# Forty-six instead of forty-one key blocks of a PEER layer sent through DRAM, and the row schedule set to match

## The chip, the core and the metric

One NeuronCore of a Trainium2 chip runs the whole kernel as a single program. Its engines are TensorE (PE in the profile; PEld is its weight load), VectorE (DVE), ScalarE (ACT), GpSimd (POOL) and SyncE (SP, which only issues transfers); each takes its instructions in order from a queue of its own, and they wait for each other and for DMA transfers through semaphores. The metric is the device time of one execution in microseconds (us), the median of several runs.

## The reference, cut to what matters

The kernel computes two transformer blocks on 512 tokens of width 1024; the change touches only the last layer of the second block, a PEER layer (a mixture of 16,384 experts of one neuron each). For every token it picks 128 experts with gates `gb`, and computes

```
u_sel = jnp.take(peer_u, eb, axis=0)              # rows of peer_u, 16384 x 1024
z     = jnp.einsum('td,tkd->tk', hb, u_sel)
act   = jax.nn.gelu(z, approximate=False) * gb
y2    = jnp.einsum('tk,tkd->td', act, jnp.take(peer_v, eb, axis=0))
```

The kernel treats the 512 tokens in two ways. For the first 384 it does not gather: it multiplies with all 16,384 experts, whose gates are zero where an expert was not picked. For the last 128 tokens it gathers the 128 rows of `peer_u` and of `peer_v` of each token.

## The kernel before

The 16,384 experts are 128 blocks ("keys") `a` of 128 experts.

**First product** (`zed(a)`, L1950). z of block `a` for 384 tokens: 24 matmuls of 128x384 into one PSUM tile `acc` (two buffers), eight steps of three (`mm3`, L121, which splits fp32 operands into a high and a low part), with a `yield` after each step. The weight comes through `weight()` (L108): SP loads `wraw` (512 KB, L105), ACT makes the high part `whi` (L117), DVE or POOL the low part `wlo` (L118). Each of the three has four slots, shared by all weights in the order of the program. ACT evicts `acc` through Gelu: for `a` below NR = 128 - ND into one of NZ = 17 tiles `zg` that stay on the chip (L1959), for the ND last blocks into `z_out` (L1962), which SP stores to DRAM as `p_zd` (L1974).

**Gates.** For each group of 16 tokens `peer_gates` (L1891) makes a dense tile `stage` of gates (128 x 128 x 16) and queues its store to DRAM, `p_gd`, 24 stores of 1 MB in all.

**What runs ahead.** The generator `zeds` (L1976) computes the ND blocks of the DRAM route and then the first NZ: 58 first products, 464 steps. `peer_pick` draws 64 + 56 + 28 + 28 = 176 steps between its instructions, `peer_gates` 276, and what is left, 12 steps, runs after the gates in the loop at L2026. Each start of a new product first loads the weight of the next one (L1981) and then issues the stores that have queued up (L1983); the last `p_gd` store is among them.

**The loop over the 128 blocks** (L2074). `fetch(a)` (L2043) brings the gates: every eighth block ACT's queue issues `gt`, 1.5 MB read back from `p_gd`, which waits for the stores. Then POOL multiplies z with the gates (`hid`, L2054), ACT and DVE split it (`hid_h` L2059, `hid_l` L2060), and the **second product** is 18 matmuls of 128x512 (`y`, six PSUM tiles that accumulate over all 128 blocks) against a block of `peer_v`, also through `weight()`. For `a` from NR on, z is read back from `p_zd` (`z_in`, L2052). As long as `a + NZ < NR`, each pass also computes the first product of block `a + NZ`, since `zg[a % NZ]` has just come free. So the loop has a first part of NR - NZ = 70 passes with both products and a second of 58 with the second product alone.

**Rows.** Each pass also handles rows of the 128 gathered tokens: POOL gathers `gu` (a row of `peer_u` per token) and `gv` (of `peer_v`), 512 KB each (L1994), DVE does the dot product (L2003) and the weighted sum into `y3` (L2035). `upto` (L2040) spreads the 128 rows: FAST = 110 of them over the first part of the loop, the rest over the second.

All instructions are ordered by a planner that simulates the engines from a cost model; the order of the program text is the priority, and `issue_after` holds an instruction behind another. The order in each engine's queue is fixed before the kernel runs.

Of the kernel before, what the change touches and what calls it, by code (L numbers as in the profile page):

```python
# [25 lines left out]
class Net:  # L26
# [1906 lines left out]
    def peer_layer(self, x, mod):  # L1933
        nc, A = self.nc, self.A
        V = nc.vector
        NZ, ND, FAST, LEAD = 17, 41, 110, 20
        xr = self.dram.tile([T, D], F32, name="p_xr")
        gd = self.dram.tile([24, 128, 128, 16], F32, name="p_gd")
        zd = self.dram.tile([ND, 128, 384], F32, name="p_zd")
# [360 lines left out]
```

## Time and profile before

| | us |
|---|---|
| median of 3 runs | 3050.35 |
| the runs | 3048.65, 3050.35, 3057.16 |
| the profiled execution | 3048.28 |
| its span in the trace | 3046.4 |
| mean granted TensorE clock | 0.954 |
| PE / DVE / ACT / POOL busy | 2748.0 / 2342.8 / 1400.3 / 1235.6 |

All places in time below are us from the start of that span. The first products run from 1845 us on (first eviction to `z_out`), the gates end near 2176, the loop runs from there to about 3005. Busy time of PE counts a pipelined matmul to its modelled end, so counts of matmuls in a stretch say more than its busy time. PEclk is the granted clock: 1.00 is 2.4 GHz, 0.5 is 1.2 GHz. "DMA share" is the mean busy share of the core's 16 DMA engines.

### The profile page before, as it was taken

How to read it: one execution, taken by the hardware profiler on the slowest of the kernel's cores; microseconds unless marked ns; L12 is line 12 of the kernel's file. 1: busy time of each engine (PE TensorE's matmuls, PEld its weight loads, DVE VectorE, ACT ScalarE, POOL GpSimd, SP SyncE). 2: the span in 40 equal slices, each digit the busy share in tenths (PEclk: the TensorE clock that was granted, in tenths of full speed). 3: DMA queues.
4: the chain of work that ended last, by engine and by line, in shares of the span. 5: the costliest groups of instructions: out<-in, count | busy, mean ns of one | idle time of the engine just before them, and what ended most of it. 6: DMA issues, size and time to landing. Idle time of an engine off the chain costs nothing.

```text
span 3046.4 us, 42674 instructions
## 1 busy us (share of the span) xinstructions
PE 2748.0 (90%) x14989; PEld 2234.8 (73%) x14989; DVE 2342.8 (77%) x4500; ACT 1400.3 (46%) x2688; POOL 1235.6 (41%) x894
## 2 busy tenths in 40 slices
PE   2899978898889798899898899999899999999996
PEld 2777556676556566576676588999889999998885
DVE  7998457768974686777974699998598888886667
ACT  3354437744554574432333533688533333333332
POOL 3111017743211484004941245120177777774332
PEclk9999889999899799998998999999999999999998
DMA  6776158933634797221011124796699999997782
GB/s 217 245 231 198 42 212 293 330 132 125 190 126 151 244 341 241 90 73 28 5 59 57 69 83 128 228 316 219 214 363 350 351 356 351 349 351 270 247 265 98
DMA packets 234337, 627.53 MB, mean 206 GB/s; under 512 B 33180, under 2 KB 95948, under 8 KB 230648
## 3 DMA queue, kind: packets, MB, share of 16 engines
q1 hardware_dynamic: 134416, 434.54, 42.0%
q0 software_dynamic: 45120, 154.42, 14.4%
q10 hardware_dynamic: 54568, 35.66, 4.0%
q8 instruction: 122, 2.00, 0.3%
q14 instruction: 111, 0.91, 0.1%
HBM read 564.94 MB, written 63.37 MB: 206 GB/s over the span
## 4 chain that ended last, share of the span: by engine, by line
PE 47%; DVE 13%; DMA 3%; issue 2%; ACT 1%; POOL 0%; POOLq 0%; DVEq 0%; ACTq 0%; SPq 0%
PE acc L124 7%; PE acc L125 7%; PE acc L126 7%; PE y L126 6%; PE y L125 6%; PE y L124 5%; DVE s_y L1367 1%; DMA wraw<-in_moe_w_gu_dram 1%; PE S L1922 1%; PE tr L1922 1%; DVE wlo L118 1%; DMA wraw<-in_moe_w_dn_dram 1%; DVE s_y L1526 1%; DVE wc L1550 1%; DVE t L1774 1%
## 5 line engine op out<-in xcount | busy, mean ns | idle before, releaser
L118 DVE TENSOR_TENSOR wlo<-wraw,whi 128x1024 fp32r<-128x1024 f32 x442 | 620.2, 1414 | 202.9 <-ACT whi L117 198.7
L117 ACT ACTIVATE whi<-wraw 128x1024 fp32r<-128x1024 f32 (+1 forms) x552 | 576.6, 1050 | 415.8 <-PE acc L125 254.3
L124 PE MATMUL acc<-h_hi,whi 128*128 128x384 f32 (+1 forms) x1328 | 475.8, 359 | 12.2 <-ACT z_out L1962 7.5
L126 PE MATMUL acc<-h_hi,wlo 128*128 128x384 f32 (+1 forms) x1328 | 466.6, 351 | 2.2 <-DVE wlo L118 2.2
L125 PE MATMUL acc<-h_lo,whi 128*128 128x384 f32 (+1 forms) x1328 | 468.1, 353 | 0.0
L118 POOL TENSOR_TENSOR wlo<-wraw,whi 128x1024 fp32r<-128x1024 f32 (+1 forms) x110 | 278.8, 2542 | 325.8 <-ACT whi L117 317.7
L124 PE MATMUL y<-whi,hid_h 128*128 128x512 f32 x768 | 299.8, 391 | 8.0 <-ACT hid_h L2059 8.0
L126 PE MATMUL y<-whi,hid_l 128*128 128x512 f32 x768 | 303.0, 395 | 4.2 <-DVE hid_l L2060 4.2
L125 PE MATMUL y<-wlo,hid_h 128*128 128x512 f32 x768 | 302.4, 394 | 0.0
L1994 POOL DMA_INDIRECT gu<-in_peer_u_dram,e x128 | 196.0, 1531 | 243.2 <-DVE gu L2003 172.5
L124 PEld LDWEIGHTS acc<-h_hi,whi 128*128 128x128 f32 x1328 | 251.5, 190 | 30.4 <-ACT z_out L1962 8.4
L126 PEld LDWEIGHTS acc<-h_hi,wlo 128*128 128x128 f32 x1328 | 251.1, 189 | 16.7 <-DVE wlo L118 2.5
L1994 POOL DMA_INDIRECT gv<-in_peer_v_dram,e x128 | 200.1, 1563 | 155.1 <-DVE stage L1927 105.6
L125 PEld LDWEIGHTS acc<-h_lo,whi 128*128 128x128 f32 x1328 | 251.5, 189 | 15.7 <-issue 0.8
L2059 ACT ACTIVATE hid_h<-hid 128x384 fp32r<-128x384 f32 x128 | 67.1, 524 | 286.6 <-PE y L125 263.5
L2035 DVE SCALAR_TENSOR_TENSOR y<-gv,pz,y 128x1024 f32<-128x1024 f32 x128 | 183.5, 1434 | 0.7 <-DMA gv<-in_peer_v_dram,e 0.6
L182 DVE SCALAR_TENSOR_TENSOR ada_w<-ada_w,silu 128x1024 f32<-128x1024 f32 x138 | 174.3, 1263 | 7.8 <-DMA ada_w<-in_w_ada_dram 7.8
L124 PEld LDWEIGHTS y<-whi,hid_h 128*128 128x128 f32 x768 | 145.0, 189 | 38.0 <-ACT hid_h L2059 8.4
L126 PEld LDWEIGHTS y<-whi,hid_l 128*128 128x128 f32 x768 | 145.1, 189 | 33.9 <-DVE hid_l L2060 4.6
L125 PEld LDWEIGHTS y<-wlo,hid_h 128*128 128x128 f32 x768 | 145.0, 189 | 31.1 <-DVE wlo L118 0.3
L2003 DVE SCALAR_TENSOR_TENSOR gu<-gu,hrow 128x1024 f32<-128x1024 f32 x128 | 162.7, 1272 | 5.4 <-DMA gu<-in_peer_u_dram,e 5.4
L124 PE MATMUL acc<-whi,h_hi 128*128 128x256 f32 x480 | 140.6, 293 | 28.4 <-ACT whi L117 18.7
(671 smaller groups left out, 6231.5 us busy)
## 6 DMA issues: line engine op xcount, KB each, us to landing
ada_w<-in_w_ada_dram SPq DMA_DIRECT2D x144, 512.0 KB
wraw<-in_moe_w_gu_dram SPq DMA_DIRECT2D x128, 512.0 KB
wraw<-in_peer_ut_dram SPq DMA_DIRECT2D x128, 512.0 KB
wraw<-in_peer_v_dram SPq DMA_DIRECT2D x128, 512.0 KB
wraw<-in_moe_w_dn_dram SPq DMA_DIRECT2D x64, 512.0 KB
p_gd<-stage SPq DMA_DIRECT2D x24, 1024.0 KB
gt<-p_gd ACTq DMA_DIRECT2D x16, 1536.0 KB
wraw<-in_fox_w_in_dram SPq DMA_DIRECT2D x24, 512.0 KB
```

Of the source, the lines that this page charges most:

```text
L117: nc.scalar.activation(hi[:, :w], r[:, :w], AF.Copy)
L118: self.low = eng.tensor_tensor(lo[:, :w], r[:, :w], hi[:, :w].bitcast(F32), op=OP.subtract).ins
L124: mm(out=out, lhsT=l[0], rhs=r[0], start=start, stop=False)
L125: mm(out=out, lhsT=l[0], rhs=r[1], start=False, stop=False)
L126: mm(out=out, lhsT=l[1], rhs=r[0], start=False, stop=stop)
L182: V.scalar_tensor_tensor(r, r, 1.0, c, op0=OP.mult, op1=OP.mult, accum_out=m)
L1367: V.scalar_tensor_tensor(acc[:, c, :], *tap(n), acc[:, c, :], op0=OP.mult, op1=OP.add)
L1922: nc.tensor.matmul(out=pt[:, t * 128:(t + 1) * 128], lhsT=a2[:, b * 4 + t, :], rhs=a1[:, b * 4 + t, :], start=True, stop=True)
L1994: nc.gpsimd.indirect_dma_start(out=u, out_offset=None, in_=src[:, :], in_offset=bass.IndirectOffsetOnAxis(ap=e3[:, k:k + 1], axis=0))
L2003: V.scalar_tensor_tensor(u, u, 1.0, hrow, op0=OP.mult, op1=OP.mult, accum_out=z8[b][:, k % 8:k % 8 + 1])
L2035: V.scalar_tensor_tensor(y3, vs.pop(k), z8[k // 8][:, k % 8:k % 8 + 1], y3, op0=OP.mult, op1=OP.add)
L2059: nc.scalar.activation(hh, hid, AF.Copy)
```

## The change

ND goes from 41 to 46, and FAST from 110 to 104.

```
-        NZ, ND, FAST, LEAD = 17, 41, 110, 20
+        NZ, ND, FAST, LEAD = 17, 46, 104, 20
```

So NR = 128 - ND goes from 87 to 82, `p_zd` holds 46 blocks, the generator has 63 first products (504 steps), of which `peer_pick` and `peer_gates` draw 452 as before; 52 are left for the loop at L2026. The first part of the main loop has 65 passes instead of 70, the second 63 instead of 58.

## Rows read from the trace of the kernel before

**Rows 1.** Busy time by stretch: stretch, us, PE, PEld, DVE, ACT, POOL, PEclk, DMA share, GB/s

```profile
2050.00:2150.00 100.00, 100.00 (x689) 100.00 (x688) 83.41 (x87) 81.99 (x217) 3.58 (x3) 1.00 0.62 221
...
2180.00:2190.00 10.00, 7.47 (x41) 6.83 (x39) 2.92 (x4) 2.50 (x3) 0.00 (x0) 1.00 0.86 263
2190.00:2200.00 10.00, 3.51 (x8) 2.82 (x9) 2.89 (x3) 0.90 (x2) 4.64 (x4) 0.52 0.39 117
2200.00:2210.00 10.00, 5.84 (x27) 4.67 (x25) 4.61 (x5) 1.59 (x2) 8.44 (x9) 0.97 1.03 370
2210.00:2220.00 10.00, 10.00 (x41) 8.46 (x40) 7.94 (x9) 3.54 (x6) 7.62 (x6) 0.83 1.03 402
...
2260.00:2300.00 40.00, 40.00 (x206) 36.53 (x205) 34.69 (x40) 13.81 (x20) 30.05 (x21) 1.00 1.00 366
...
2600.00:2700.00 100.00, 100.00 (x508) 90.95 (x508) 81.60 (x94) 35.38 (x50) 73.06 (x50) 1.00 0.99 352
...
2900.00:2950.00 50.00, 50.00 (x220) 41.03 (x219) 33.62 (x29) 18.20 (x26) 19.43 (x16) 1.00 0.88 281
```

**Rows 2.** All waits of PE between 2160 and 2230 us: total, times, longest

```profile
PE y L124 <- ACT hid_h L2059: 8.0, 1, 8.0
PE y L126 <- DVE hid_l L2060: 4.2, 1, 4.2
PE acc L124 <- ACT whi L117: 1.0, 1, 1.0
```

**Rows 3.** Timeline around the loop's start: start us, duration, instruction [idle before <-releaser]

```profile
2173.82 0.83 PE L1922 MATMUL tr<-a,a 128*128 128x128 f32 x6
...
2176.17 0.33 SPq L1974 DMA_DIRECT2D p_gd<-stage  x1
...
2178.23 1.06 ACT L117 ACTIVATE whi<-wraw 128x1024 fp32r<-128x1024 f32 x1 [3.57 <-PE acc L125]
...
2182.25 0.38 ACTq L2046 DMA_DIRECT2D gt<-p_gd  x1
...
2186.71 1.06 ACT L117 ACTIVATE whi<-wraw 128x1024 fp32r<-128x1024 f32 x1 [2.60 <-PE acc L125]
2187.82 0.44 PE L124 MATMUL acc<-h_hi,whi 128*128 128x384 f32 x1 [0.97 <-ACT whi L117]
...
2194.89 0.99 POOL L2054 TENSOR_TENSOR hid<-x,gt 128x384 f32<-128x384 f32 x1 [27.88 <-DMA gt<-p_gd]
...
2196.03 0.99 POOL L1994 DMA_INDIRECT gu<-in_peer_u_dram,e  x1
...
2196.47 0.56 DVE L2060 TENSOR_TENSOR hid_l<-hid,hid_h 128x384 fp32r<-128x384 f32 x1 [9.95 <-ACT hid_h L2059]
2196.49 0.80 PE L124 MATMUL y<-whi,hid_h 128*128 128x512 f32 x1 [8.05 <-ACT hid_h L2059]
...
2204.79 2.45 DVE L2003 SCALAR_TENSOR_TENSOR gu<-gu,hrow 128x1024 f32<-128x1024 f32 x1 [5.43 <-DMA gu<-in_peer_u_dram,e]
...
2209.05 0.55 DVE L2060 TENSOR_TENSOR hid_l<-hid,hid_h 128x384 fp32r<-128x384 f32 x1
```

**Rows 4.** PE's groups by shape: 2180 to 2240, 2300 to 2700, 2800 to 2950 us

```profile
L124 PE MATMUL acc<-h_hi,whi 128*128 128x384 f32 x43 | 14.6, 339 | 1.0 <-ACT whi L117 1.0
...
L124 PE MATMUL y<-whi,hid_h 128*128 128x512 f32 x30 | 13.4, 447 | 8.0 <-ACT hid_h L2059 8.0
...
L124 PE MATMUL acc<-h_hi,whi 128*128 128x384 f32 x384 | 128.8, 335 | 0.0
...
L124 PE MATMUL y<-whi,hid_h 128*128 128x512 f32 x292 | 113.4, 388 | 0.0
...
L124 PE MATMUL y<-whi,hid_h 128*128 128x512 f32 x219 | 85.0, 388 | 0.0
```

**Rows 5.** Evictions of first products, by source line: count, duration ns min/median/max

```profile
L1962 ACT ACTIVATE z_out<-acc x41: 464/475/493, 1845.3 to 2072.4; 128x384 f32<-128x384 f32 x41
...
L1959 ACT ACTIVATE zg<-acc x35: 463/472/493, 2147.4 to 2765.2; 128x384 f32<-128x384 f32 x35
```

## The prediction

> **What bounds the kernel now.** I read the busy time by stretch first, because the change moves work between stages, and an average over the span says nothing about either. Before the loop's start (2050 to 2150 us) PE is busy all the time at full clock; so it is in the loop's first part (2600 to 2700) and in its second (2900 to 2950) [rows 1]. In these stages TensorE sets the pace, and DVE, ACT and POOL have room. Between 2180 and 2220 it is not so: PE's four rows hold 41, 8, 27 and 41 matmuls in 10 us each, where the loop's first part holds 508 in 100, and the granted clock falls to 0.52 and again to 0.83 [rows 1].
>
> The waits name the hole. PE waits three times: 8.05 us for `hid_h` of the first block, 4.2 us for the `hid_l` of the second, 1.0 for a weight, 13.2 in all [rows 2]. The timeline gives the chain behind it [rows 3]: the last gates' matmuls end at 2174.65, the last `p_gd` store is issued at 2176.17, `gt` can be issued at 2182.25, it has landed when POOL starts `hid` at 2194.89 (12.6 us), and the first second product starts at 2196.49. That is 22 us after the gates, in which PE has only the 12 left steps and the first products of the loop that fit the two `acc` buffers.
>
> The size of the hole comes from counts [rows 4]. Each shape stands there in three rows of equal or nearly equal count; one of each is shown. In the second part 3 x 219 = 657 `y` matmuls take 150 us: 0.2283 us each. In the first part 3 x 292 = 876 `y` and 3 x 384 = 1152 `acc` matmuls take 400 us: (400 - 876 x 0.2283) / 1152 = 0.1736 us each. So one first product costs 24 x 0.1736 = 4.17 us, one second product 18 x 0.2283 = 4.11, a pass with both 8.28. Between 2180 and 2240 there are 127 `acc` (43 + 42 + 42) and 90 `y` matmuls, worth 22.05 + 20.55 = 42.6 us. The stretch is 60 us long, so **17.4 us are lost**: 13.2 of waits and some 4.2 at the lower clock (1.2 GHz), which follows the idle time.
>
> **The change part by part.**
>
> *Five first products leave the loop and run after the gates.* The work is the same: 5 x 24 matmuls, 20.8 us, less in the loop and more before it. The gates draw as many steps as before, so all of it lands at L2026: 52 steps of three matmuls, 27.1 us instead of 6.2. From 2174.65 PE is then busy until 2201.7, against 2196.49 when the first second product can start. The first wait (8.05), the small one (0.97) and the low clock after them go. What it takes: five weights more in that stretch, each one SP load, one `whi` and one `wlo`. The four slots let them run ahead: in the trace `whi` is made as soon as a first product frees a slot (2178.23 and 2186.71, both released by PE [rows 3]), three products before its use.
>
> *The wait behind the blocked queues.* ACT stands at `hid_h` and DVE at `hid_l` (9.95 us of idle time) until `gt` has landed [rows 3]; any `whi` or `wlo` that the planner places behind them waits too. In this trace `hid_h` stands behind the `whi` of 2186.71, 12.1 us after the gates. If the planner keeps that distance, the third of the six whole left products is running then and the weights up to the sixth are made or just being made; PE has work until about 2201.7 and ACT is free again at 2196.5. So cost 0. The other bound is that `hid_h` comes directly after the gates: then four weights are ready, 16.7 us of work, until 2191.3, and PE stands for the 5 us to 2196.5 and some 2 more for the next weight. I take the first, since the order in the trace is nearest to it.
>
> *`gt` among more transfers.* Up to four more `wraw` loads (2.1 MB) run beside it. At 366 GB/s [rows 1] they take 5.7 us; if all of it delays `gt`, the second products can start at 2202.2, about when PE ends the left ones. Lower bound 0. The last `p_gd` store now stands behind the load of a next weight on SP (L1981 before L1983); that load waits at most for one product, 4.2 us. Either delay alone is nearly covered. I take 1.5 us for both.
>
> *The second wait (4.2 us).* DVE waited 5.43 us for gathered rows issued at 2196.03 and used at 2204.79, and `hid_l` of the second block stood behind them until 2209.05 [rows 3]. With the change `y` of block 0 runs from about 2202 to 2206, the first product of block 17 (done inside the hole before) to 2210, and only then is the second `hid_l` wanted. So it is covered by about a microsecond; if the order puts the second product first, 3 us of it stay.
>
> *Five more blocks through DRAM.* The eviction costs ACT 475 ns instead of 472 [rows 5]. Five stores and five loads of 197 KB are 2 MB, at 366 GB/s 5.4 us of DMA time, the stores beside the gates at a share of 0.62, the loads in the second part at 0.88, PE busy throughout in both [rows 1]: cost nothing; without that cover at most 5.4 us.
>
> *The rows.* First part: 104 / 65 = 1.600 per pass instead of 110 / 70 = 1.571, 1.8% more. DVE is busy 81.6 and POOL 73.1 of 100 us there [rows 1], so even if all of it were rows they would go to 83.1 and 74.4: no new bound. Second part: 24 rows over 61 passes (0.39) instead of 18 over 56 (0.32), at most 23% more on DVE's 33.6 of 50: 41.3 of 50. Nothing.
>
> *DMA in the first part.* Bytes of a pass: two weights of 524,288, an eighth of `gt` 196,608, and 1.571 pairs of rows of 2 x 524,288, 2.893 MB in 8.28 us, 349 GB/s; the row of 2600 to 2700 says 352 at a share of 0.99 [rows 1]. With 1.6 it is 2.923 MB, 353 GB/s. The same queues moved 366 over 40 us and 402 over 10 us [rows 1] with PE busy throughout from 2260 on. I take it as hidden: at 366 a pass needs 7.99 us of DMA, under 8.28.
>
> Against this stands a rule of the Trainium skill, page "DMA: Bandwidth & Descriptors", section Specifications: it puts the HBM limit of one core at about 358 GB/s. By it a pass would need 8.16 us, still under the pace of PE, so the sum would be the same, but with 1.4% of room where the row of 366 leaves 3.5%; it would put the DMA rival below higher. The trace has exceeded that figure twice, so I go by the rows.
>
> **Sum.** 17.4 recovered, less 1.5 for a wait that remains: 15.9 us. 3048.28 - 15.9 = 3032.4 for the profiled execution, which is 2.1 us below the median of the runs shown, 3050.35; as median I give **3033**.
>
> **Rivals.**
>
> *The second wait stays* (with its lower clock). For it: the gathers still start only after the first `hid`, and took 8.8 us. Against: PE has one product more before it needs them. Price 4.2 + 1.6 us of lower clock, and up to 4 more if `gt` lands late too: gain 8 to 12, 3037 to 3041.
>
> *The left products don't fill the hole.* If the planner puts `hid_h`, `hid_l` or the `gt` issue in front of weights that the left products need, PE stands as before and the five products run after it; the loop is shorter by as much. Against: the order in this trace. Gain 0 to 4: 3044 to 3050.
>
> *Slower: DMA paces the loop's first part.* For it: a share of 0.99 to 1.00, and in the hole, where DMA had a share of only 0.39 for 10 us [rows 1], it could catch up so far. The place is each of 65 passes. The gain is eaten when a pass needs 8.28 + 15.9 / 65 = 8.52 us, that is from 343 GB/s down; at 335, 5% under the 352 of the trace, a pass is 8.73 us, 29 us more over 65 passes, 13 over the gain: 3061. Against: 366 and 402 were reached.
>
> **How the numbers follow.** Chances: hole closed 0.66 (3030 to 3036), second wait stays 0.15, hole not filled 0.11, DMA-paced 0.08. A change under 0.3% (9.2 us) can't be told from none. Faster by more than that, under 3041.2: the first case and nearly all of the second, 0.80. Within: the third and a rest, 0.13. Slower: most of the fourth, 0.07. The range of 8 in 10 holds the first two cases and a little of the third: 3029 to 3045. Its lower end is the full 17.4 and two microseconds of scatter.
>
> **What would show it.** Right: some 165 `acc` matmuls without a wait after the last gates' matmul, the clock at 1.00 between 2180 and 2220, the first `y` matmul near 2202 to 2204 with no wait on `hid_h`, first-part passes still 8.28 us with 508 matmuls in 100 us, and the gain all before 2260. Wrong: `hid_h` idle time of ACT followed by a wait of PE for `whi` or `wlo` inside the left products; waits of PE for `hid_l` after the first passes; a granted clock under 1.00 later in the loop; or any wait of PE in the first part.

## The result, and the profile after

The changed kernel takes 3034.45 us (median of five runs, 3032.78 to 3041.73), the kernel before 3050.35 (five runs, 3046.99 to 3061.44): ratio 0.9942, 95% interval 0.9921 to 0.9964, or 17.7 us less (11 to 24). The forecast was 3033, in a range of 3029 to 3045.

The profiled execution of the changed kernel took 3041.73 us, the slowest of its five; its span is 3039.7, only 6.7 us under that of before. Its profile shows both why the change works and why this execution shows less of it.

Busy time by stretch, the stretches of [rows 1] (stretch, us, PE, PEld, DVE, ACT, POOL, PEclk, DMA share, GB/s):

```profile
2050.00:2150.00 100.00, 100.00 (x690) 100.00 (x689) 82.51 (x85) 82.66 (x219) 2.44 (x2) 1.00 0.64 224
...
2180.00:2190.00 10.00, 10.00 (x59) 10.00 (x58) 2.36 (x2) 2.73 (x4) 1.25 (x2) 1.00 0.86 254
2190.00:2200.00 10.00, 10.00 (x57) 9.68 (x56) 6.40 (x7) 4.03 (x8) 8.79 (x8) 1.00 0.90 299
2200.00:2210.00 10.00, 9.58 (x48) 8.32 (x47) 9.44 (x10) 6.01 (x9) 5.99 (x5) 1.00 1.05 389
2210.00:2220.00 10.00, 10.00 (x50) 8.92 (x49) 7.70 (x10) 1.57 (x3) 8.62 (x7) 1.00 0.93 338
...
2260.00:2300.00 40.00, 40.00 (x201) 36.20 (x200) 34.86 (x39) 13.66 (x21) 27.04 (x21) 1.00 1.01 363
...
2600.00:2700.00 100.00, 100.00 (x500) 90.70 (x499) 84.74 (x97) 35.27 (x50) 75.23 (x51) 1.00 0.95 337
...
2900.00:2950.00 50.00, 50.00 (x216) 40.51 (x215) 34.03 (x29) 17.30 (x24) 19.35 (x16) 1.00 0.83 266
```

Between 2180 and 2220 there are 214 matmuls where before had 117, and the granted clock stays at 1.00 (2.4 GHz). But the loop's rows show 500 matmuls in 100 us where before had 508, at the same granted clock and with PE busy throughout. That second difference is not a wait; the experiments come back to it.

All waits of PE between 2160 and 2230 us, against three of 13.2 us in [rows 2]:

```profile
PE acc L126 <- DVE wlo L118: 0.4, 1, 0.4
```

The timeline around the loop's start, against [rows 3], put together from the engines' own timelines:

```profile
2169.08 1.05 PE L1922 MATMUL tr<-a,a 128*128 128x128 f32 x8
...
2171.80 0.33 SPq L1974 DMA_DIRECT2D p_gd<-stage  x1
...
2178.38 0.38 ACTq L2046 DMA_DIRECT2D gt<-p_gd  x1
...
2182.76 2.00 ACT L117 ACTIVATE whi<-wraw 128x1024 fp32r<-128x1024 f32 x2
...
2188.61 1.02 POOL L2054 TENSOR_TENSOR hid<-x,gt 128x384 f32<-128x384 f32 x1 [26.12 <-DMA wraw<-in_peer_ut_dram]
...
2189.66 0.52 ACT L2059 ACTIVATE hid_h<-hid 128x384 fp32r<-128x384 f32 x1 [4.90 <-POOL hid L2054]
...
2189.77 0.98 POOL L1994 DMA_INDIRECT gu<-in_peer_u_dram,e  x1
...
2190.53 1.05 ACT L117 ACTIVATE whi<-wraw 128x1024 fp32r<-128x1024 f32 x1
...
2194.06 0.54 DVE L2060 TENSOR_TENSOR hid_l<-hid,hid_h 128x384 fp32r<-128x384 f32 x1
...
2199.26 0.39 PE L124 MATMUL y<-whi,hid_h 128*128 128x512 f32 x1
```

The gates end at 2170.1, `hid_h` of the first block is made at 2189.66, and PE takes it up at 2199.26, having run 164 `acc` matmuls since the gates without a wait. The 0.4 us of the view above come only after the first second product, for the low part of a weight of the loop:

```profile
2204.33 0.44 PE L126 MATMUL acc<-h_hi,wlo 128*128 128x384 f32 x1 [0.42 <-DVE wlo L118]
```

`hid_h` now waits for PE, no longer PE for `hid_h`. ACT still stands for 4.90 us in front of it, but the weights that PE needs meanwhile lie ready. `hid_l` of the second block (2194.06) is done before the first second product begins; DVE makes it ahead of the first dot product behind the gates, where before it stood behind one [rows 3]:

```profile
2195.73 1.22 DVE L2003 SCALAR_TENSOR_TENSOR gu<-gu,hrow 128x1024 f32<-128x1024 f32 x1
```

PE's groups by shape, 2180 to 2240, 2300 to 2700 and 2800 to 2950 us, against [rows 4] (of three rows for each shape one is shown):

```profile
L124 PE MATMUL acc<-h_hi,whi 128*128 128x384 f32 x73 | 24.8, 339 | 0.0
...
L124 PE MATMUL y<-whi,hid_h 128*128 128x512 f32 x30 | 11.9, 396 | 0.0
...
L124 PE MATMUL acc<-h_hi,whi 128*128 128x384 f32 x378 | 127.8, 338 | 0.0
...
L124 PE MATMUL y<-whi,hid_h 128*128 128x512 f32 x286 | 113.6, 397 | 0.0
...
L124 PE MATMUL y<-whi,hid_h 128*128 128x512 f32 x215 | 85.4, 397 | 0.0
```

In the same 60 us there are 219 `acc` and 90 `y` matmuls, before 127 and 90: 92 more, 16.0 us at 0.1736 each. That is the gain, as far as one window of 60 us can tell it. In the 400 us of the first part there are 1136 `acc` and 857 `y` instead of 1152 and 876, in the second part 645 `y` instead of 657: 1.7% and 1.8% less work per time. Over the loop of some 810 us this takes back 14 us in this one execution.

### The profile page after: what moved, and what is told of

It reads as the page before. It is cut to its first block, busy times and chain, and to the rows that moved or that the text cites. A ratio compares the mean times of both kernels' runs of the same rounds, so it can differ in the third digit from the quotient of the medians.

```text
span 3039.7 us, 42702 instructions
## 1 busy us (share of the span) xinstructions
PE 2755.4 (91%) x14989; PEld 2242.6 (74%) x14989; DVE 2347.9 (77%) x4500; ACT 1399.2 (46%) x2688; POOL 1238.5 (41%) x894
## 4 chain that ended last, share of the span: by engine, by line
PE 47%; DVE 13%; DMA 4%; issue 2%; ACT 1%; POOL 0%; POOLq 0%; DVEq 0%; ACTq 0%; SPq 0%
PE acc L124 7%; PE acc L125 7%; PE acc L126 7%; PE y L125 6%; PE y L124 6%; PE y L126 6%; DMA wraw<-in_moe_w_dn_dram 2%; DMA wraw<-in_moe_w_gu_dram 2%; DVE s_y L1367 1%; PE S L1922 1%; PE tr L1922 1%; DVE s_y L1526 1%; DVE wlo L118 1%; DVE wc L1550 1%; DVE t L1774 1%
## 5 line engine op out<-in xcount | busy, mean ns | idle before, releaser
L124 PEld LDWEIGHTS acc<-h_hi,whi 128*128 128x128 f32 x1328 | 252.3, 190 | 27.8 <-ACT z_out L1962 6.8
L125 PEld LDWEIGHTS acc<-h_lo,whi 128*128 128x128 f32 x1328 | 252.5, 190 | 15.9 <-issue 0.9
L124 PE MATMUL acc<-whi,h_hi 128*128 128x256 f32 x480 | 141.2, 294 | 27.3 <-ACT whi L117 18.7
```

The source lines that it names most:

```text
L124: mm(out=out, lhsT=l[0], rhs=r[0], start=start, stop=False)
L125: mm(out=out, lhsT=l[0], rhs=r[1], start=False, stop=False)
```

## The experiments

Two theories stood at the start. **A**: the gain is the hole of TensorE before the loop, filled by the products left over. **B**: it comes from the row schedule, which asks less of DMA and VectorE per time. Each ratio below, with its 95% interval, stands against runs of the kernel before on the same chip; the microseconds beside it are the ratio's, taken on the median of those runs.

**The five products without the rows.**

```
-        NZ, ND, FAST, LEAD = 17, 41, 110, 20
+        NZ, ND, FAST, LEAD = 17, 46, 110, 20
```

> ND 46, FAST left at 110: five more first products before the loop, rows not spread to match (110 over 65 passes, 1.69 per pass). Theory A (the gain is the hole of TensorE before the loop, filled): as fast as the changed kernel, 14 to 17 us under before; no wait of PE for hid_h; 2180 to 2240 holds about 309 matmuls instead of 217. Theory B (the gain comes from the slower row schedule, which relieves DMA and VectorE): no gain, since rows per pass are now more than before.

Ratio 0.9958 (0.9942 to 0.9974): 12.8 us less (8 to 18), a little under the 14 to 17 expected but not apart from them. The one wait of PE near the loop's start is 0.4 us. Its stretches 2180 to 2240 and 2300 to 2700 us:

```profile
2180.00:2240.00 60.00, 59.57 (x312) 55.32 (x311) 46.37 (x50) 22.97 (x34) 41.08 (x31) 1.00 0.97 332
2300.00:2700.00 400.00, 400.00 (x2028) 364.06 (x2027) 356.68 (x402) 141.95 (x203) 306.71 (x213) 1.00 1.00 369
```

A holds, B falls: the gain comes without the row schedule. The second row also answers the DMA rival. With 1.69 rows per pass this kernel moved 369 GB/s over 400 us at a share of 1.00, and PE ran as many matmuls as in before.

**The rows without the products.**

```
-        NZ, ND, FAST, LEAD = 17, 41, 110, 20
+        NZ, ND, FAST, LEAD = 17, 41, 104, 20
```

> ND 41, FAST 104: only the row schedule (1.49 rows per pass over 70 passes). Theory A: no change, within 3 us of before, the hole of 17 us still there (PE waits of 8 us for hid_h and some 4 for hid_l). Theory B: most of the gain, 10 us or more.

Ratio 0.9986 (0.9968 to 1.0004): no difference that can be told, though the interval reaches from 10 us less to 1 us more. The waits of PE, and DVE's timeline behind the first of them:

```profile
PE y L124 <- ACT hid_h L2059: 7.2, 1, 7.2
PE acc L124 <- ACT whi L117: 1.0, 1, 1.0
```

```profile
2199.56 0.56 DVE L2060 TENSOR_TENSOR hid_l<-hid,hid_h 128x384 fp32r<-128x384 f32 x1 [8.79 <-ACT hid_h L2059]
...
2203.91 0.56 DVE L2060 TENSOR_TENSOR hid_l<-hid,hid_h 128x384 fp32r<-128x384 f32 x1 [1.47 <-ACT hid_h L2059]
...
2208.96 1.22 DVE L2003 SCALAR_TENSOR_TENSOR gu<-gu,hrow 128x1024 f32<-128x1024 f32 x1
```

The first wait is there, the second (4.2 us for `hid_l`) is gone, against the expectation. With 104 rows over 70 passes the second pass has one row instead of two (2 x 104 / 70 is under 3), and in this kernel's order the second `hid_l` (2203.91) stands in front of the dot product that waits for gathered rows (2208.96); in before it stood behind it [rows 3]. Which step of the planner turns the order isn't shown. So the row schedule is not quite nothing: with the hole open it removes its smaller wait. From the table below an estimate of its worth is 6 us (840.5 us at 2019 matmuls, brought to the pace of 2028 by half the difference between 832.3 and 828.0). That is a part of the same hole, and not a relief of DMA or VectorE in the loop.

**The first gates at hand.** The first eight blocks take a resident tile instead of `gt` (their gates are left out), so nothing at the loop's start waits for DRAM. One of the 16 loads of `gt` goes with it.

```
-                    if a % 8 == 0:
+                    if a % 8 == 0 and a:
...
-   z.rearrange("p (b t) -> p b t", t=16), gt[0][:, :, a % 8, :],
+   z.rearrange("p (b t) -> p b t", t=16), gt[0][:, :, a % 8, :] if a >= 8 else h[0][:, 0, :384].bitcast(F32).rearrange("p (b t) -> p b t", t=16),
```

> ND 41, FAST 110, but the first eight blocks are multiplied with a tile that is on the chip anyway instead of gates read back from DRAM (leaves out the gates of the first eight blocks). Theory A: the hole is the chain p_gd store, gt load, hid; without it PE goes from the gates to the loop with no wait on hid_h, and the kernel is 13 to 17 us under before although no product was moved. Theory B: no change.

> The same with ND 46, FAST 104 (gates of the first eight blocks left out). Theory A: there is no hole to fill, so the five moved products bring nothing more: within 3 us of the same kernel with ND 41. Theory B: about 16 us under that one. On the pace of the matmuls in the loop, which was 508 per 100 us in the profile of before and 500 in that of the change with no wait in either: if the idle time before the loop sets it, all kernels without the hole show 500; if it is drawn anew in each execution, some of them show 508.

Ratios 0.9951 (0.9933 to 0.9969) with ND 41 and 0.9955 (0.9939 to 0.9971) with ND 46. With ND 41, `hid` starts right after the gates, whose last matmul ends at 2183.7 in this execution, and PE has one wait of 1.0 us left:

```profile
2183.88 1.62 POOL L2054 TENSOR_TENSOR hid<-x,h_hi 128x384 f32<-128x384 f32 x1 [7.80 <-ACT zg L1959]
```

```profile
PE y L124 <- ACT hid_h L2059: 1.0, 1, 1.0
```

Taking the chain away brings 15 us without moving a product, and then the five products bring nothing more that can be told. Both halves of A are shown: the hole is the way of the gates through DRAM, and the moved products gain only by filling it.

**The changed kernel and the kernel before again.**

> The changed kernel once more, beside the others on one chip. Theory A: 13 to 17 us under before. Pace of the loop: 500 matmuls per 100 us, as in its first profile, if the pace belongs to the program; possibly another (505 to 508) if it is drawn in each execution.

> The kernel before once more, for a second profile. The hole of 17 us and the three waits of PE as in the first. Pace of the loop: 508 per 100 us if it belongs to the program or follows from the hole, another if it is drawn in each execution.

The change again: 0.9951 (0.9934 to 0.9967), 15.0 us less (10 to 20). Before again has its hole, with three waits as in [rows 2]:

```profile
PE y L124 <- ACT hid_h L2059: 7.9, 1, 7.9
PE y L126 <- DVE hid_l L2060: 4.5, 1, 4.5
PE acc L124 <- ACT whi L117: 1.0, 1, 1.0
```

**Two and ten more instead of five.**

```
-        NZ, ND, FAST, LEAD = 17, 41, 110, 20
+        NZ, ND, FAST, LEAD = 17, 43, 107, 20
```

> ND 43, FAST 107 (68 passes): two products more are left over, 28 steps, 14.6 us after the gates. Theory A: about 8 us of the hole are filled, the first wait for hid_h shrinks to under 2 us, the wait for the second hid_l may stay: 8 to 13 us under before. Theory B' (the gain is proportional to the products moved out of the loop): two fifths of it, 6 us.

```
-        NZ, ND, FAST, LEAD = 17, 41, 110, 20
+        NZ, ND, FAST, LEAD = 17, 51, 98, 20
```

> ND 51, FAST 98 (60 passes): ten products more are left over, 92 steps, 48 us after the gates. Theory A: the hole is full at 46, so nothing more is gained: within 4 us of the changed kernel. Theory B': twice its gain, about 30 us under before.

Two more: 0.9966 (0.9946 to 0.9986), 10.4 us less (4 to 16). Two waits remain:

```profile
PE y L124 <- ACT hid_h L2059: 2.2, 1, 2.2
PE acc L126 <- DVE wlo L118: 0.5, 1, 0.5
```

The interval of two more also holds the 6 us of B'; the table below, at equal pace, has 12.5 us less for it (831.8 against 844.3), where B' asks for two fifths of 16.3, or 6.5. Ten more: 0.9959 (0.9939 to 0.9978), 12.5 us less (7 to 19), not twice the gain of five. The gain grows until the hole is full and then stays. None of these versions can be told from the change by its time.

**Second and third profiles, for the pace.** The profile of ND 51 had the shortest span of all, that of the change one of the longer ones without the hole, with under 1 us of wait in either.

> ND 46, FAST 110 once more, for a second profile: in the first the loop's part of both products ran 2028 matmuls in 400 us (2300 to 2700), the changed kernel 1999 and 2010. If the pace belongs to the program: within 5 of 2028 again. If it is drawn in each execution: it may come out at 2000 to 2015. No wait of PE for hid_h in either case.

> The changed kernel a third time: if the pace belongs to the program, 1995 to 2015 matmuls in 2300 to 2700; if it is drawn in each execution, 2020 to 2032 is as likely. The hole stays closed.

> ND 51, FAST 98 once more, for a second profile: its first had 2030 matmuls in 2300 to 2700. Program: within 5 of it. Execution: anything from 1999 to 2032, and a slower pace goes with a longer time, some 12 us for 1.5%.

Two of these expectations name 1999 matmuls for the first profile of the change; the count is 1993. The row of 2300 to 2700 us, first for ND 46 with FAST 110 in its second profile (its first, above, has 2028), then for ND 51 in its first and second:

```profile
2300.00:2700.00 400.00, 400.00 (x2008) 363.99 (x2008) 350.22 (x397) 141.19 (x202) 303.00 (x209) 1.00 0.99 363
```

```profile
2300.00:2700.00 400.00, 400.00 (x2030) 364.15 (x2029) 344.96 (x392) 142.64 (x203) 296.24 (x206) 1.00 0.98 358
```

```profile
2300.00:2700.00 400.00, 400.00 (x2011) 364.28 (x2010) 343.69 (x390) 141.74 (x202) 299.26 (x205) 1.00 0.97 354
```

The same program runs 2028 or 2008, 2030 or 2011, so the program alone does not set the pace. The chip alone doesn't either: the chip of the first four experiments showed 2028, 2019, 2009 and 2011, that of the next four 2010, 2028, 2029 and 2030, in four kernels each. But the second profile of each of these two programs was taken on another chip than its first; that the pace is drawn in each execution, and does not belong to a program on one chip, is not shown. All profiles together, worked out from their timelines (gates' end: end of the last matmul of L1922; first and last y: starts; the counts are from the rows of 2300 to 2700; waits of PE near the loop's start):

| kernel | span | gates' end | to first y | to last y | matmuls in 400 us | waits |
|---|---|---|---|---|---|---|
| before | 3046.4 | 2174.7 | 21.8 | 844.3 | 2028 | 13.2 |
| before, again | 3046.0 | 2174.1 | 21.7 | 844.4 | 2028 | 13.3 |
| rows alone | 3046.6 | 2178.6 | 21.0 | 840.5 | 2019 | 8.2 |
| gates at hand, 41 | 3044.8 | 2183.7 | 12.0 | 833.5 | 2009 | 1.0 |
| gates at hand, 46 | 3036.6 | 2176.8 | 29.0 | 832.3 | 2011 | 0 |
| ND 43 | 3036.0 | 2176.8 | 18.7 | 831.8 | 2029 | 2.7 |
| ND 46 alone | 3025.2 | 2169.4 | 29.2 | 828.0 | 2028 | 0.4 |
| ND 46 alone, again | 3032.5 | 2172.4 | 29.0 | 832.3 | 2008 | 0 |
| the change | 3039.7 | 2170.1 | 29.1 | 842.1 | 1993 | 0.4 |
| the change, again | 3036.0 | 2176.2 | 29.0 | 832.3 | 2010 | 0 |
| the change, third | 3037.7 | 2177.7 | 29.0 | 832.5 | 2010 | 0 |
| ND 51 | 3023.2 | 2167.7 | 50.8 | 828.1 | 2030 | 0.7 |
| ND 51, again | 3038.6 | 2178.7 | 50.3 | 832.4 | 2011 | 0 |

From the last y to the end it is 27.5 to 27.8 us in all of them. So a span is the sum of three parts. The first is the time to the gates' end, before which all these kernels run the same 10,961 matmuls; it varies by 16 us from profile to profile, and no difference between ND 41 (2174.1 to 2183.7) and ND 46 (2169.4 to 2177.7) can be told in it. The second is the part to the last y, which holds the hole; in before it ends at 2174.7 + 844.3 = 3019.0, so the loop runs to there and not to about 3005. The third is the end.

At the pace of before (2028 to 2030) a kernel without the hole needs 828.0 or 828.1 us from the gates to the last y, before 844.3 or 844.4: **16.3 us less**. At 2008 to 2011 the change, ND 46 alone, ND 51 and the gates at hand with ND 46 all need 832.3 to 832.5. No profile of the change itself fell on the pace of 2028; that it would then need 828 too is inferred from these.

## Why the prediction was right

**The size of the hole.** 17.4 us were counted out of 60 us of one profile. At equal pace the profiles give 16.3, the two timed comparisons of the change 17.7 and 15.0. The forecast was 15.9. That it comes so near is partly luck: the count is 1.1 us above what was found at equal pace, and 1.5 us were taken off for a delay that did not come. The median is closer still by chance: 3050.35 - 15.9 would be the 3034.45 measured, the forecast took 3033 without saying why, and the five runs spread over 9 us.

**The five products after the gates.** Predicted: some 165 `acc` matmuls without a wait, the first `y` at 2202 to 2204 (27 to 29 us after the gates), the clock at 1.00. The runs: 164 matmuls, 29.0 to 29.2 us after the gates (at 2199.26 in the first profile, whose gates ended earlier), no wait before the first `y`, 1.00. One reading was wrong: of the two `whi` that were to be made three products before their use, that of 2186.71 was used at 2187.82, and PE had waited 0.97 us for it [rows 3]. It did no harm, as the change's weights were there in time. That the lower clock belonged to the idle time is borne out: with the wait the two falls of PEclk are gone.

**The blocked queues.** ACT stood 4.90 us before `hid_h`, and the weights behind it came in time but for 0.4 us after the first second product. `hid_h` stands behind the two `whi` of 2182.76, 12.6 us after the gates, where the trace of before had 12.1, so taking its end of the bounds was right. With two products more instead of five the same chain left 2.2 us.

**`gt` among more transfers** was the term that was mis-sized, 1.5 us taken and none needed: from its issue at 2178.38 to `hid` at 2188.61 are 10.2 us, where before took 12.6, and in the other executions of the change 9.2 and 9.5. (In the first and third of them the profile names the load of a weight, not `gt`, as what ended POOL's wait, so these are times to the use; the landing of `gt` itself isn't shown.) Made at 2189.66 and used at 2199.26, `hid_h` had 9.6 us to spare. The store of the last gates was issued 1.7 us after their last matmul, before 1.5; the load that the program text puts before it on SP cost nothing.

**The second wait** was to be covered by a microsecond, if the order held. It was covered by more, and the order did not hold. The second `hid_l` is made at 2194.06, before the first second product begins: the gates land while PE still runs first products, and it now stands ahead of the dot product. Even behind it (2195.73 and 1.22 us) it would have been ready 11 us before the second block's product, which starts 38.2 us after the gates, at 2208.3. The order is turned in every kernel with products moved, ND 46 with FAST 110 among them, although their second pass has two rows as in before.

**Five more blocks through DRAM.** The evictions cost the same, 474 ns against [rows 5] (first of its columns: count, then min, median, max):

```profile
L1962 ACT ACTIVATE z_out<-acc x46: 459/474/495, 1840.7 to 2101.6; 128x384 f32<-128x384 f32 x46
```

**The rows** were put at nothing. Inside the change that holds: with FAST at 110 the same hole closes and the loop needs the same time at the same pace. By themselves they moved one `hid_l` ahead of a dot product, which the prediction did not see, since it looked at rates per pass and not at which pass gets its second row.

**The DMA rival** is ruled out in this range: 369 GB/s held for 400 us with TensorE at full pace. The rule that spoke against the change, of the Trainium skill's page "DMA: Bandwidth & Descriptors" (section Specifications, about 358 GB/s of HBM for one core), is exceeded here; the measurement decides.

**What it missed:** passes of 8.28 us with 508 matmuls in 100, which it had named as a sign of being right. No profile of the change shows them: the first has passes of 42 / 1993 x 400 = 8.43 us, the others 8.36, so part of the gain made before 2260 is lost again later. That this is not the change is taken from its neighbours: before has 8.28 twice, ND 46 alone and ND 51 have 8.28 and 8.36, and ND 41 with the gates at hand 8.36.

## What to carry to other kernels

Where one engine is saturated on both sides of a hand-over through DRAM, count its instructions per time there: what is missing against the steady stretch is what can be won, and independent work moved in pays until the hole is full and nothing after. Moving work costs nothing only as long as its inputs run ahead; look at which queue stands still during the wait and how many buffers are filled by then. When a profile disagrees with the median, cut the span at places that the change can't reach before explaining the difference.

## What the runs showed of the hardware

With PE busy throughout and the granted clock at 1.00, the same matmuls run at different paces: in a pass of the loop's first part 8.28 us (2028 to 2030 matmuls in 400 us), 8.32 (2019), 8.36 (2008 to 2011) or 8.43 (1993). Start to start, worked out from PE's timelines, a 128x384 matmul takes 173.4, 174.7 or 176.7 ns there in the mean, and a 128x512 one 229 to 230; only in the first profile of the change it takes 233, and that in the second part as well (216 matmuls in 50 us, before 220). Each pace held over the whole first part of an execution; ND 46 alone had 173.4 in one profile and 176.7 in the other. From 2000 us to the gates' end all profiles have a median of 177. Neither the hole (ND 46 alone and ND 51 have both paces without it), nor the row schedule, nor the DMA traffic (2028 stand beside 369 GB/s, 2011 beside 354) explains it; what does stays open, and so does whether it changes between executions on one chip. It is worth 4 to 14 us here, as much as the change.
